# A row-wise softmax over 4096 rows of 32768: from four partitions per row to one whole row per partition

## Chip, cores and metric

One Trainium2 chip, one of its cores. The metric is device microseconds (us) of one execution; lower is better. All runs told here were with a granted clock of 1.000. In the profiles DVE is VectorE, ACT is ScalarE, and SPq is the sequencer that issues the transfers; "the page" is the summary of one profiled execution. Code is condensed, and cuts are marked with `...`.

## The reference

```
logits: (16, 256, 32768) float32, temperature = 1.0
scaled = logits / temperature
scaled = scaled - scaled.max(axis=-1, keepdims=True)
e = exp(scaled)
return e / e.sum(axis=-1, keepdims=True)      # float32
```

Flattened, that is 4096 rows of 128 KB: 537 MB in and 537 MB out. A row that was read once and stays in on-chip memory until it is scaled needs no second read, and both kernels work so.

## The kernel before

Each row is cut into four parts of 8192 elements, which lie on four neighbouring partitions. A tile is 32 rows, 128 partitions of 32 KB, or 4 MiB that lie together in memory. A tile finishes its own rows, so it can be stored as soon as it has been computed; the four partitions of a row exchange their maxima and sums by shuffles.

```
_W = 8192; _BUFS = 6; _AHEAD = 4; _CC = 4096; _SCALE_ON_DVE = {1, 4, 7}
x = xf.rearrange("n (h v) -> (n h) v", h=SPLIT)            # SPLIT = 4

def load(t):  nc.sync.dma_start(out=xs, in_=x[t * P : (t + 1) * P, :])
def store(t): nc.sync.dma_start(out=o[t * P : (t + 1) * P, :], in_=slots.pop(t))

def compute(t):
    for c in range(NCH):                                    # two pieces of 4096
        nc.vector.tensor_reduce(out=nm[:, c:c+1], in_=xc, axis=X, op=A.max, negate=True)
        nc.scalar.activation(out=xc, in_=xc, func=Exp, bias=nm[:, c:c+1], scale=inv_t,
                             accum_out=ssum[:, c:c+1])
    # ... small ops: maximum and sum over the pieces, combine() over four partitions,
    # reciprocal, factor f per piece ...
    for c in range(NCH):
        if (t * NCH + c) % 8 in _SCALE_ON_DVE:
            nc.vector.tensor_scalar_mul(out=xc, in0=xc, scalar1=f[:, c:c+1])
        else:
            nc.scalar.activation(out=xc, in_=xc, func=Copy, scale=f[:, c:c+1])

for t in range(min(_AHEAD, n_tiles)): load(t)
for t in range(n_tiles):
    compute(t); store(t)
    if t + _AHEAD < n_tiles: load(t + _AHEAD)
```

Of the kernel before, what the change touches and what calls it, by code (L numbers as in the profile page):

```python
# [1 line left out]

# [4 lines left out]


_W = 8192
_BUFS = 6  # L10
_AHEAD = 4
_CC = 4096
_SCALE_ON_DVE = {1, 4, 7}


@with_exitstack
def kernel(
    ctx: ExitStack,
    tc: tile.TileContext,
    logits: bass.AP,  # L20
    temperature: bass.AP,
    out: bass.AP,
):
    nc = tc.nc
    inv_t = 1.0 / float(temperature)
    P = nc.NUM_PARTITIONS
    fp32 = mybir.dt.float32
    Exp = mybir.ActivationFunctionType.Exp
    Copy = mybir.ActivationFunctionType.Copy
    X = mybir.AxisListType.X  # L30
    A = mybir.AluOpType

    xf = logits.flatten_outer_dims()
    of = out.flatten_outer_dims()
    N, V = xf.shape
    W = min(_W, V)
    SPLIT = V // W
    assert SPLIT * W == V and (N * SPLIT) % P == 0 and W % _CC == 0
    x = xf.rearrange("n (h v) -> (n h) v", h=SPLIT)
    o = of.rearrange("n (h v) -> (n h) v", h=SPLIT)  # L40
    n_tiles = N * SPLIT // P
    n_rounds = SPLIT.bit_length() - 1
    NCH = W // _CC

    xpool = ctx.enter_context(tc.tile_pool(name="x", bufs=_BUFS))
    spool = ctx.enter_context(tc.tile_pool(name="stats", bufs=8))
    slots = {}

    def load(t: int) -> None:
        xs = xpool.tile([P, W], fp32, tag="x", name="xs")  # L50
        slots[t] = xs
        tc.keep_in_program_order(
            nc.sync.dma_start(out=xs, in_=x[t * P : (t + 1) * P, :])
        )

    def store(t: int) -> None:
        tc.keep_in_program_order(
            nc.sync.dma_start(out=o[t * P : (t + 1) * P, :], in_=slots.pop(t))  # L58
        )

    def combine(v, op) -> None:
        for j in range(n_rounds):
            mask = [i ^ (1 << j) for i in range(32)]
            nc.vector.stream_shuffle(  # L64
                out=v[:, j + 1 : j + 2], in_=v[:, j : j + 1], mask=mask
            )
            nc.vector.tensor_tensor(  # L67
                out=v[:, j + 1 : j + 2],
                in0=v[:, j : j + 1],
                in1=v[:, j + 1 : j + 2],  # L70
                op=op,
            )

    def compute(t: int) -> None:
        xs = slots[t]
        nm = spool.tile([P, NCH], fp32, tag="nm", name="nm")
        ssum = spool.tile([P, NCH], fp32, tag="ssum", name="ssum")
        ee = spool.tile([P, NCH], fp32, tag="ee", name="ee")
        f = spool.tile([P, NCH], fp32, tag="f", name="f")
        ttj = spool.tile([P, NCH], fp32, tag="ttj", name="ttj")  # L80
        nMh = spool.tile([P, 1 + n_rounds], fp32, tag="nMh", name="nMh")
        Sh = spool.tile([P, 1 + n_rounds], fp32, tag="Sh", name="Sh")
        rS = spool.tile([P, 1], fp32, tag="rS", name="rS")

        for c in range(NCH):
            xc = xs[:, c * _CC : (c + 1) * _CC]
            nc.vector.tensor_reduce(  # L87
                out=nm[:, c : c + 1], in_=xc, axis=X, op=A.max, negate=True
            )
            if inv_t != 1.0:  # L90
                nc.vector.tensor_scalar_mul(
                    out=nm[:, c : c + 1], in0=nm[:, c : c + 1], scalar1=inv_t
                )
            nc.scalar.activation(  # L94
                out=xc,
                in_=xc,
                func=Exp,
                bias=nm[:, c : c + 1],
                scale=inv_t,
                accum_out=ssum[:, c : c + 1],  # L100
            )

        with tc.high_priority():
            nc.vector.tensor_reduce(out=nMh[:, 0:1], in_=nm, axis=X, op=A.min)  # L104
            combine(nMh, A.min)
            nc.scalar.activation(  # L106
                out=ee,
                in_=nm,
                func=Exp,
                bias=nMh[:, n_rounds : n_rounds + 1],  # L110
                scale=-1.0,
            )
            nc.vector.tensor_tensor_reduce(  # L113
                out=ttj,
                in0=ee,
                in1=ssum,
                scale=1.0,
                scalar=0.0,
                op0=A.mult,
                op1=A.add,  # L120
                accum_out=Sh[:, 0:1],
            )
            combine(Sh, A.add)
            nc.vector.reciprocal(out=rS, in_=Sh[:, n_rounds : n_rounds + 1])  # L124
            nc.scalar.activation(out=f, in_=ee, func=Copy, scale=rS)  # L125

        for c in range(NCH):
            xc = xs[:, c * _CC : (c + 1) * _CC]
            if (t * NCH + c) % 8 in _SCALE_ON_DVE:
                nc.vector.tensor_scalar_mul(out=xc, in0=xc, scalar1=f[:, c : c + 1])  # L130
            else:
                nc.scalar.activation(out=xc, in_=xc, func=Copy, scale=f[:, c : c + 1])  # L132

    for t in range(min(_AHEAD, n_tiles)):
        load(t)
    for t in range(n_tiles):
        compute(t)
        store(t)
        if t + _AHEAD < n_tiles:
            load(t + _AHEAD)  # L140


# [1 line left out]
_INS = ['logits', 'temperature']  # L144
_OUTS = [((16, 256, 32768), 'float32')]

_NUMBERS = {'temperature': 1.0}


# [26 lines left out]
```

## Time and profile before

| | before |
|---|---|
| median (range), runs at prediction time | 2506.95 us (2502.8 to 2507.95) |
| DMA queue, share of 16 engines' span | 99.6% |
| DVE, ACT busy | 63%, 65% |
| rate in the middle | 433 GB/s |

These are lines of the page of the kernel before: the span, the engines' busy time, the DMA share in tenths and the rate in 40 equal slices, the DMA queue (packets, MB, share), the chain of waits by engine, and three groups of instructions (line, engine, operation, shapes, count; busy us and mean ns; idle time just before, and its releaser).

```profile
span 2500.8 us, 4102 instructions
...
DVE 1564.4 (63%) x2400; ACT 1625.0 (65%) x929; POOL 0.2 (0%) x4
...
DMA  9999999999999999999999999999999999999997
GB/s 406 429 432 431 431 434 433 431 434 434 431 436 433 431 435 433 432 434 432 432 436 431 432 435 433 432 435 433 431 435 433 431 435 433 431 435 433 431 434 325
...
q1 hardware_dynamic: 36864, 1073.76, 99.6%
...
DMA 76%; DVE 10%; ACT 8%; another core or an unknown queue 4%; issue 0%; SPq 0%; ACTq 0%
...
L87 DVE TENSOR_REDUCE nm<-xs 128x1 f32<-128x4096 f32 x256 | 1119.6, 4414 | 432.9 <-DMA xs<-in_logits_dram 432.9
...
L132 ACT ACTIVATE xs<-xs,f 128x4096 f32<-128x4096 f32 x160 | 589.9, 3705 | 4.1
...
L130 DVE TENSOR_SCALAR xs<-xs,f 128x4096 f32<-128x4096 f32 x96 | 225.9, 2353 | 41.0 <-ACT f L125 39.7
```

The DMA row stands at 9 in all slices but the last, and the rate hardly moves: the kernel is bound by the DMA engines. DVE waits 433 us for loads, which costs nothing.

A table of windows of the same kernel has, per stretch, its length, the busy us of each engine, the clock, the DMA share and the rate.

```profile
core 0: us, DVE busy (x) ACT busy (x) POOL busy (x), PEclk, DMA share, GB/s
...
1000.00:2400.00 1400.00, 880.70 (x1350) 912.54 (x522) 0.00 (x0) 1.00 1.00 433
2475.00:2501.00 26.00, 2.30 (x1) 3.65 (x1) 0.00 (x0) 1.00 0.45 192
```

In the middle the engines move 433 GB/s at a share of 1.00; one 4 MiB transfer takes 9.68 us. The last 26 us are less than half used: the last load must be reduced, exponentiated and scaled before the last store. The Trainium skill, "DMA: Bandwidth & Descriptors", section "Where 436 GB/s comes from", gives a fabric ceiling of 435.2 GB/s; this trace agrees. (The same section says that some 358 GB/s, a core's half of its HBM stack, bind transfers between HBM and on-chip memory; with one core at work, as here, they did not.) So no change to the computation can gain much in the middle.

The timeline of one tile (start, duration, engine, line, operation) gives the length of what stands between a landed load and its store:

```profile
999.33 8.74 DVE L87 TENSOR_REDUCE nm<-xs 128x1 f32<-128x4096 f32 x2 [2.63 <-DMA xs<-in_logits_dram]
...
1013.37 0.29 ACT L125 ACTIVATE f<-ee,rS 128x2 f32<-128x2 f32 x1 [1.27 <-DVE rS L124]
1013.70 3.71 ACT L132 ACTIVATE xs<-xs,f 128x4096 f32<-128x4096 f32 x1
1013.70 2.35 DVE L130 TENSOR_SCALAR xs<-xs,f 128x4096 f32<-128x4096 f32 x1 [0.42 <-ACT f L125]
1017.43 0.34 SPq L58 DMA_DIRECT2D out_dram<-xs  x1
```

From the first reduce (999.33) to the store's issue (1017.43) are 18.1 us. Nothing waits for them, because four loads are ahead.

### The profile page before, as it was taken

How to read it: one execution, taken by the hardware profiler on the slowest of the kernel's cores; microseconds unless marked ns; L12 is line 12 of the kernel's file. 1: busy time of each engine (PE TensorE's matmuls, PEld its weight loads, DVE VectorE, ACT ScalarE, POOL GpSimd, SP SyncE). 2: the span in 40 equal slices, each digit the busy share in tenths (PEclk: the TensorE clock that was granted, in tenths of full speed). 3: DMA queues.
4: the chain of work that ended last, by engine and by line, in shares of the span. 5: the costliest groups of instructions: out<-in, count | busy, mean ns of one | idle time of the engine just before them, and what ended most of it. 6: DMA issues, size and time to landing. Idle time of an engine off the chain costs nothing.

```text
span 2500.8 us, 4102 instructions
## 1 busy us (share of the span) xinstructions
DVE 1564.4 (63%) x2400; ACT 1625.0 (65%) x929; POOL 0.2 (0%) x4
## 2 busy tenths in 40 slices
DVE  6666566666566665666666666666666666666564
ACT  6766666666666666666666666666666666666664
POOL 0000000000000000000000000000000000000000
DMA  9999999999999999999999999999999999999997
GB/s 406 429 432 431 431 434 433 431 434 434 431 436 433 431 435 433 432 434 432 432 436 431 432 435 433 432 435 433 431 435 433 431 435 433 431 435 433 431 434 325
DMA packets 36896, 1074.02 MB, mean 429 GB/s; under 512 B 4096, under 2 KB 4096, under 8 KB 4096
## 3 DMA queue, kind: packets, MB, share of 16 engines
q1 hardware_dynamic: 36864, 1073.76, 99.6%
q14 instruction: 32, 0.26, 0.0%
HBM read 536.87 MB, written 536.87 MB: 429 GB/s over the span
## 4 chain that ended last, share of the span: by engine, by line
DMA 76%; DVE 10%; ACT 8%; another core or an unknown queue 4%; issue 0%; SPq 0%; ACTq 0%
DMA xs<-in_logits_dram 47%; DMA out_dram<-xs 29%; DVE nm L87 9%; ACT xs L132 4%; ACT xs L94 4%; DVE Sh L67 0%; DVE Sh L64 0%; ACT f L125 0%; ACT ee L106 0%; DVE rS L124 0%; DVE ttj L113 0%; SPq L58 0%; DVE xs L130 0%; DVE nMh L67 0%
## 5 line engine op out<-in xcount | busy, mean ns | idle before, releaser
L87 DVE TENSOR_REDUCE nm<-xs 128x1 f32<-128x4096 f32 x256 | 1119.6, 4414 | 432.9 <-DMA xs<-in_logits_dram 432.9
L94 ACT ACTIVATE xs<-xs,nm 128x4096 f32<-128x4096 f32 x256 | 949.1, 3707 | 677.5 <-DVE nm L87 677.5
L132 ACT ACTIVATE xs<-xs,f 128x4096 f32<-128x4096 f32 x160 | 589.9, 3705 | 4.1
L113 DVE CUSTOM_DVE_ANT_0 ttj<-ee,ssum 128x2 f32<-128x2 f32 x128 | 20.5, 160 | 391.5 <-ACT ee L106 382.9
L130 DVE TENSOR_SCALAR xs<-xs,f 128x4096 f32<-128x4096 f32 x96 | 225.9, 2353 | 41.0 <-ACT f L125 39.7
L125 ACT ACTIVATE f<-ee,rS 128x2 f32<-128x2 f32 x128 | 37.8, 295 | 159.0 <-DVE rS L124 159.0
L94 ACT ACTIVATION_READ_ACCUMULATOR xs<-xs,nm 128x1 f32 x256 | 47.7, 187 | 0.0
L67 DVE TENSOR_TENSOR nMh<-nMh 128x1 f32<-128x1 f32 x256 | 40.8, 159 | 8.6
L67 DVE TENSOR_TENSOR Sh<-Sh 128x1 f32<-128x1 f32 x256 | 40.8, 159 | 8.6
L64 DVE STREAM_SHUFFLE nMh<-nMh 128x1 f32<-128x1 f32 x256 | 38.8, 151 | 0.0
L64 DVE STREAM_SHUFFLE Sh<-Sh 128x1 f32<-128x1 f32 x256 | 38.7, 151 | 0.0
L106 ACT ACTIVATE ee<-nm,nMh 128x2 f32<-128x2 f32 x128 | 35.8, 280 | 0.0
L124 DVE RECIPROCAL rS<-Sh 128x1 f32<-128x1 f32 x128 | 21.0, 164 | 4.3
L104 DVE TENSOR_REDUCE nMh<-nm 128x1 f32<-128x2 f32 x128 | 19.8, 155 | 4.3
L113 DVE DVE_READ_ACCUMULATOR2_ANT Sh<- 128x1 f32 x128 | 10.6, 83 | 0.0
L64 DVE LOAD_MASK_SELECT Sh<-Sh x256 | 3.6, 14 | 10.8
L64 DVE LOAD_MASK_SELECT nMh<-nMh x256 | 3.6, 14 | 10.8
L94 ACT ACT_TABLE_LOAD x1 | 1.3, 1283 | 13.1 <-DMA xs<-in_logits_dram 13.1
L157 POOL MEMSET const-bfloat16-1.0<- 128x1 bf16 x1 | 0.1, 101 | 0.0
L157 POOL MEMSET const-uint8-127<- 128x1 uint8 x1 | 0.1, 101 | 0.0
L157 POOL MEMSET const-float32-0.0<- 128x1 f32 x1 | 0.1, 98 | 0.2 <-issue 0.2
L157 POOL MEMSET const-float32-1.0<- 128x1 f32 x1 | 0.1, 98 | 0.0
## 6 DMA issues: line engine op xcount, KB each, us to landing
xs<-in_logits_dram SPq DMA_DIRECT2D x128, 4096.0 KB, 48.4
out_dram<-xs SPq DMA_DIRECT2D x128, 4096.0 KB, 49.6
```

Source lines behind the costliest of these rows:

```text
L64: nc.vector.stream_shuffle(out=v[:, j + 1 : j + 2], in_=v[:, j : j + 1], mask=mask)
L67: nc.vector.tensor_tensor(out=v[:, j + 1 : j + 2], in0=v[:, j : j + 1], in1=v[:, j + 1 : j + 2], op=op,)
L87: nc.vector.tensor_reduce(out=nm[:, c : c + 1], in_=xc, axis=X, op=A.max, negate=True)
L94: nc.scalar.activation(out=xc, in_=xc, func=Exp, bias=nm[:, c : c + 1], scale=inv_t, accum_out=ssum[:, c : c + 1],)
L104: nc.vector.tensor_reduce(out=nMh[:, 0:1], in_=nm, axis=X, op=A.min)
L106: nc.scalar.activation(out=ee, in_=nm, func=Exp, bias=nMh[:, n_rounds : n_rounds + 1], scale=-1.0,)
L113: nc.vector.tensor_tensor_reduce(out=ttj, in0=ee, in1=ssum, scale=1.0, scalar=0.0, op0=A.mult, op1=A.add, accum_out=Sh[:, 0:1],)
L124: nc.vector.reciprocal(out=rS, in_=Sh[:, n_rounds : n_rounds + 1])
L125: nc.scalar.activation(out=f, in_=ee, func=Copy, scale=rS)
L130: nc.vector.tensor_scalar_mul(out=xc, in0=xc, scalar1=f[:, c : c + 1])
L132: nc.scalar.activation(out=xc, in_=xc, func=Copy, scale=f[:, c : c + 1])
L157: nc = _bacc.Bacc("TRN2", target_bir_lowering=False, num_devices=1)
```

## The change

Each partition holds a whole row in four chunks of 32 KB (a *group* is 128 rows, four chunks), so no exchange between partitions is needed. All four chunks must have been exponentiated before any can be scaled and stored. Six buffers hold one and a half groups. Each scale is split between DVE (2560 columns) and ACT (1536). A transfer takes 128 pieces of 32 KB at a pitch of 128 KB. The loads of the first and last groups and the stores of the last move in half transfers, to start and end sooner. Two small edits come with it: the factors are computed on DVE instead of ACT, and the small statistics tiles have three buffers instead of eight.

```
-_W = 8192
+_SPLIT = 1
+_CW = 8192
 _BUFS = 6
-_AHEAD = 4
-_CC = 4096
-_SCALE_ON_DVE = {1, 4, 7}
+_PIECE = 4096
+_LAST_DMA = 4096
+_DVE_SHARE = 0.625
 ...
+    def load(i):
+        g, c = divmod(i, C)                                  # C = 4 chunks per group
+        for s, n in spans(CW, _LAST_DMA if g in (0, G - 1) else CW):
+            nc.sync.dma_start(out=xs[:, s : s + n],
+                in_=x[g * P : (g + 1) * P, c * CW + s : c * CW + s + n])
 ...                                       (store alike, halves in the last group only)
+            cut = int(n * _DVE_SHARE) // 512 * 512
+            nc.vector.tensor_scalar_mul(out=xs[:, s : s + cut], ...)
+            nc.scalar.activation(out=xs[:, s + cut : s + n], ..., func=Copy, ...)
 ...
+    order = [("L", i) for i in range(min(_BUFS, n_chunks))] + [("S", 0)]
+    for i in range(1, n_chunks):
+        order.append(("S", i))
+        if i + _BUFS - 1 < n_chunks:
+            order.append(("L", i + _BUFS - 1))
 ...                   (before the first "S" of a group: exps of its four chunks, then factors)
```

More of the change, by code (lines that the diff above doesn't have):

```diff
@@ L35, with spans, piece, load @@
     N, V = xf.shape
-    W = min(_W, V)
-    SPLIT = V // W
-    assert SPLIT * W == V and (N * SPLIT) % P == 0 and W % _CC == 0
-    x = xf.rearrange("n (h v) -> (n h) v", h=SPLIT)
-    o = of.rearrange("n (h v) -> (n h) v", h=SPLIT)
-    n_tiles = N * SPLIT // P
-    n_rounds = SPLIT.bit_length() - 1
-    NCH = W // _CC
+    W = V // _SPLIT
+    CW = min(_CW, W)
+    C = W // CW
+    assert W * _SPLIT == V and CW * C == W and (N * _SPLIT) % P == 0
+    x = xf.rearrange("n (h v) -> (n h) v", h=_SPLIT)
+    o = of.rearrange("n (h v) -> (n h) v", h=_SPLIT)
+    G = N * _SPLIT // P
+    n_chunks = G * C
+    n_rounds = _SPLIT.bit_length() - 1
     xpool = ctx.enter_context(tc.tile_pool(name="x", bufs=_BUFS))
-    spool = ctx.enter_context(tc.tile_pool(name="stats", bufs=8))
+    spool = ctx.enter_context(tc.tile_pool(name="stats", bufs=3))
     slots = {}
-    def load(t: int) -> None:
-        xs = xpool.tile([P, W], fp32, tag="x", name="xs")
-        slots[t] = xs
-        tc.keep_in_program_order(
-            nc.sync.dma_start(out=xs, in_=x[t * P : (t + 1) * P, :])
-        )
-    def store(t: int) -> None:
-        tc.keep_in_program_order(
-            nc.sync.dma_start(out=o[t * P : (t + 1) * P, :], in_=slots.pop(t))
-        )
+    stats = {}
+    def spans(total: int, step: int) -> list[tuple[int, int]]:
+        return [(s, min(step, total - s)) for s in range(0, total, step)]
+    def piece(g: int) -> int:
+        return _PIECE if g < G - 1 else min(_PIECE, _LAST_DMA)
+    def load(i: int) -> None:
+        g, c = divmod(i, C)
+        xs = xpool.tile([P, CW], fp32, tag="x", name="xs")
+        slots[i] = xs
+        for s, n in spans(CW, _LAST_DMA if g in (0, G - 1) else CW):
+            tc.keep_in_program_order(
+                nc.sync.dma_start(
+                    out=xs[:, s : s + n],
+                    in_=x[g * P : (g + 1) * P, c * CW + s : c * CW + s + n],
+                )
+            )
+    def store(i: int) -> None:
+        g, c = divmod(i, C)
+        xs = slots.pop(i)
+        for s, n in spans(CW, _LAST_DMA if g == G - 1 else CW):
+            tc.keep_in_program_order(
+                nc.sync.dma_start(
+                    out=o[g * P : (g + 1) * P, c * CW + s : c * CW + s + n],
+                    in_=xs[:, s : s + n],
+                )
+            )
     def combine(v, op) -> None:
@@ L72, in combine, with exps, factors @@
             )
-    def compute(t: int) -> None:
-        xs = slots[t]
-        nm = spool.tile([P, NCH], fp32, tag="nm", name="nm")
-        ssum = spool.tile([P, NCH], fp32, tag="ssum", name="ssum")
-        ee = spool.tile([P, NCH], fp32, tag="ee", name="ee")
-        f = spool.tile([P, NCH], fp32, tag="f", name="f")
-        ttj = spool.tile([P, NCH], fp32, tag="ttj", name="ttj")
+    def exps(i: int) -> None:
+        g, c = divmod(i, C)
+        xs = slots[i]
+        ps = spans(CW, piece(g))
+        K = C * len(ps)
+        if c == 0:
+            stats[g] = tuple(
+                spool.tile([P, K], fp32, tag=f"{nm}{K}", name=nm)
+                for nm in ("nm", "ssum", "ee", "f", "ttj")
+            )
+        nm, ssum = stats[g][:2]
+        for j, (s, n) in enumerate(ps):
+            k = c * len(ps) + j
+            nc.vector.tensor_reduce(
+                out=nm[:, k : k + 1], in_=xs[:, s : s + n], axis=X, op=A.max, negate=True
+            )
+            if inv_t != 1.0:
+                nc.vector.tensor_scalar_mul(
+                    out=nm[:, k : k + 1], in0=nm[:, k : k + 1], scalar1=inv_t
+                )
+            nc.scalar.activation(
+                out=xs[:, s : s + n],
+                in_=xs[:, s : s + n],
+                func=Exp,
+                bias=nm[:, k : k + 1],
+                scale=inv_t,
+                accum_out=ssum[:, k : k + 1],
+            )
+    def factors(g: int) -> None:
+        nm, ssum, ee, f, ttj = stats[g]
         nMh = spool.tile([P, 1 + n_rounds], fp32, tag="nMh", name="nMh")
@@ L83, in compute @@
         rS = spool.tile([P, 1], fp32, tag="rS", name="rS")
-        for c in range(NCH):
-            xc = xs[:, c * _CC : (c + 1) * _CC]
-            nc.vector.tensor_reduce(
-                out=nm[:, c : c + 1], in_=xc, axis=X, op=A.max, negate=True
-            )
-            if inv_t != 1.0:
-                nc.vector.tensor_scalar_mul(
-                    out=nm[:, c : c + 1], in0=nm[:, c : c + 1], scalar1=inv_t
-                )
-            nc.scalar.activation(
-                out=xc,
-                in_=xc,
-                func=Exp,
-                bias=nm[:, c : c + 1],
-                scale=inv_t,
-                accum_out=ssum[:, c : c + 1],
-            )
         with tc.high_priority():
@@ L124, in compute, with scales @@
             nc.vector.reciprocal(out=rS, in_=Sh[:, n_rounds : n_rounds + 1])
-            nc.scalar.activation(out=f, in_=ee, func=Copy, scale=rS)
-        for c in range(NCH):
-            xc = xs[:, c * _CC : (c + 1) * _CC]
-            if (t * NCH + c) % 8 in _SCALE_ON_DVE:
-                nc.vector.tensor_scalar_mul(out=xc, in0=xc, scalar1=f[:, c : c + 1])
-            else:
-                nc.scalar.activation(out=xc, in_=xc, func=Copy, scale=f[:, c : c + 1])
-    for t in range(min(_AHEAD, n_tiles)):
-        load(t)
-    for t in range(n_tiles):
-        compute(t)
-        store(t)
-        if t + _AHEAD < n_tiles:
-            load(t + _AHEAD)
+            nc.vector.tensor_scalar_mul(out=f, in0=ee, scalar1=rS)
+    def scales(i: int) -> None:
+        g, c = divmod(i, C)
+        xs = slots[i]
+        f = stats[g][3]
+        ps = spans(CW, piece(g))
+        for j, (s, n) in enumerate(ps):
+            k = c * len(ps) + j
+            cut = int(n * _DVE_SHARE) // 512 * 512
+            nc.vector.tensor_scalar_mul(
+                out=xs[:, s : s + cut], in0=xs[:, s : s + cut], scalar1=f[:, k : k + 1]
+            )
+            nc.scalar.activation(
+                out=xs[:, s + cut : s + n],
+                in_=xs[:, s + cut : s + n],
+                func=Copy,
+                scale=f[:, k : k + 1],
+            )
+    order = [("L", i) for i in range(min(_BUFS, n_chunks))] + [("S", 0)]
[3 more added lines that the diff above has]
+            order.append(("L", i + _BUFS - 1))
+    nxt = 0
+    done = -1
+    loaded = 0
+    for kind, i in order:
+        if kind == "L":
+            load(i)
+            loaded = i + 1
+        else:
+            g = i // C
+            if g > done:
+                while nxt < (g + 1) * C:
+                    assert nxt < loaded
+                    exps(nxt)
+                    nxt += 1
+                factors(g)
+                done = g
+            scales(i)
+            store(i)
 _INS = ['logits', 'temperature']
```

## The prediction

> **What bounds the kernel now.** The DMA engines. The page's second part shows them at least 90% busy in 39 of 40 slices; its third part gives the queue 99.6% of 16 engines' span, 1073.7 MB. A table of windows gives 433 GB/s at DMA share 1.00 from 100 to 2400 us. The timeline repeats one load plus one store every 19.35 to 19.40 us: 9.7 us per 4 MiB transfer. DVE (63%) and ACT (65%) have slack; the chain is 76% DMA. Little is lost at the ends: about 1.5 us idle in the first 13 us, and about 14 us in the last 26 (DMA share 0.45), where the last load is followed by reduce, exponential, factors and scale before the last store.
>
> **What the change does.**
> - Bytes and number of large transfers stay, so the floor stays near 1073.7 MB / 433 GB/s = 2480 us.
> - Removed: 512 shuffles (151 ns) and 512 combines (159 ns), 159 us of DVE; the factor chain runs 32 times, not 128. Each scale is split: DVE 2560 of 4096 columns (estimate from 2353 ns: 1.48 us), ACT 1536 (estimate from 3.7 us per 4096 and 0.28 us for two columns: 1.5 us). DVE busy about 1500 us, ACT 1360. None of this is on the critical path.
> - Added: no chunk can be stored before all four of its group are exponentiated, with six buffers; load i+5 waits until store i-1 has landed.
> - The 32 KB pieces of a transfer lie 128 KB apart.
>
> **The critical stretch.** By the new issue order, in each group the last load is followed in the queue by just one store and one load (19.4 us). In that time must fit: landing notice, two reduces and the last exponential with its accumulator (12.6 us in the old timeline), factors (about 0.9 us from the small ops), the first chunk's scale (3.05 us), issue and start. That is 16.7 us of compute; the first load's 12.27 us from issue to landing less 9.7 puts notice and start together at about 2.6 us. Sum 19.3 against 19.4: just balanced. I expect a gap of 0 to 1 us per group, 0.4 typical, times 31: about 12 us.
>
> **Ends.** At the start six loads (58 us) cover the first group's compute (first store near 54 us). At the end, half-size transfers and four stores in a row leave about 7 us idle instead of 15: 8 us gained.
>
> **Spacing.** The Trainium skill, "DMA: Bandwidth & Descriptors", section "Latency and other measured facts", has copies of 16 KiB pieces at a 512 KiB pitch at 207 GB/s per direction against 214 full, far less from 2 MiB up. 128 KB is below its smallest figure; no run here shows it yet. I allow 0 to 1%, 0.2% (5 us) typical.
>
> **Sum.** 2507 - 8 + 12 + 5 = 2516, shaded to 2512 us because the balance may leave no gap. Range 2488 to 2548. Faster by over 2% would need more than the DMA ceiling: 1%. Within 2%: 88%. Slower: 11%.
>
> **What would show it.** DMA share near 1.00 in the middle windows at 430 to 433 GB/s; DVE near 1500 and ACT near 1360 us; stores' wait for DVE or ACT ends, once per group, within about 1 us of the queue draining; less idle in the last 26 us. If DMA share is 1.00 but GB/s below 430, pieces are slower; if share falls, gaps are the cause.
>
> **What would make it wrong.** Pieces 128 KB apart several per cent slower; notice-to-start above 2.6 us under load, or engines out of step, so that gaps reach 2 us per group (over 60 us); scales on DVE and ACT together slower than alone; or a scheduler order that puts a later group's reduces before scales.

## The result

| | before | after |
|---|---|---|
| median (range) | 2505.12 us (2502.8 to 2507.95), 4 runs | 2580.66 us (2579.22 to 2581.61), 4 runs |
| ratio of the runs, 95% interval | | 1.0301 (1.0283 to 1.0318) |
| DVE, ACT busy, us | 1564, 1625 | 1518, 1359 |
| rate in the middle | 433 GB/s | 416 GB/s |

A ratio is the mean time of one kernel's runs over that of the other's of the same rounds, so it is not quite the ratio of the medians. The change made the kernel 3% slower, outside the predicted range.

The same lines of the page after the change:

```profile
span 2579.0 us, 2299 instructions
...
DVE 1517.9 (59%) x672; ACT 1359.3 (53%) x801; POOL 0.2 (0%) x4
...
DMA  9999999999999999999999999999999999999999
GB/s 415 431 430 425 413 421 416 419 413 412 415 423 416 412 410 420 414 422 412 416 417 422 418 411 412 418 422 417 411 416 416 423 417 415 410 416 423 418 410 384
...
q1 hardware_dynamic: 38592, 1073.76, 98.9%
...
DMA 96%; ACT 1%; DVE 1%; SPq 1%; issue 0%; ACTq 0%
...
L107 DVE TENSOR_REDUCE nm<-xs 128x1 f32<-128x4096 f32 x256 | 1119.7, 4413 | 901.4 <-DMA xs<-in_logits_dram 901.4
...
L163 ACT ACTIVATE xs<-xs,f 128x1536 f32<-128x1536 f32 x256 | 378.9, 1562 | 24.5 <-DVE f L150 24.5
L160 DVE TENSOR_SCALAR xs<-xs,f 128x2560 f32<-128x2560 f32 x256 | 377.3, 1548 | 1.1
```

DVE and ACT came out as predicted (1518 and 1359 us against 1500 and 1360), and the DMA row still says 9 everywhere. But the rate is near 416, and the chain is 96% DMA: the DMA engines are occupied, and deliver less. The windows agree, and show that the end improved:

```profile
1000.00:2400.00 1400.00, 831.44 (x373) 745.67 (x441) 0.00 (x0) 1.00 0.99 416
2545.00:2579.00 34.00, 2.34 (x2) 2.45 (x2) 0.00 (x0) 1.00 0.95 402
```

The timeline at the end of one group: the reduces of its last chunk, the scales, the issue of the group's first store (L75) and of the load behind it (L64):

```profile
1076.36 8.74 DVE L107 TENSOR_REDUCE nm<-xs 128x1 f32<-128x4096 f32 x2 [11.62 <-DMA xs<-in_logits_dram]
...
1089.84 7.40 DVE L160 TENSOR_SCALAR xs<-xs,f 128x2560 f32<-128x2560 f32 x5
1089.89 7.44 ACT L163 ACTIVATE xs<-xs,f 128x1536 f32<-128x1536 f32 x5 [0.77 <-DVE f L150]
1092.96 0.33 SPq L75 DMA_DIRECT2D out_dram<-xs  x1
1093.39 0.38 SPq L64 DMA_DIRECT2D xs<-in_logits_dram  x1
```

From the first reduce on the group's last chunk (1076.36) to the issue of the group's first store (1092.96) are 16.60 us; the prediction had 16.7. Now the DMA engines around that store:

```profile
1082.50:1092.20 9.70, 5.70 (x8) 8.46 (x7) 0.00 (x0) 1.00 1.00 432
1092.20:1093.70 1.50, 1.50 (x2) 1.50 (x2) 0.00 (x0) 1.00 0.07 27
1093.70:1102.00 8.30, 8.30 (x7) 8.03 (x6) 0.00 (x0) 1.00 1.03 439
1102.00:1104.10 2.10, 2.10 (x1) 0.00 (x0) 0.00 (x0) 1.00 0.97 265
1104.10:1111.20 7.10, 6.18 (x2) 4.69 (x3) 0.00 (x0) 1.00 1.03 443
1111.20:1115.00 3.80, 0.00 (x0) 2.91 (x2) 0.00 (x0) 1.00 1.00 302
1115.00:1124.70 9.70, 6.72 (x2) 2.27 (x1) 0.00 (x0) 1.00 0.99 429
```

The view counts a piece in the stretch in which it starts, so that a share can exceed 1.00. The second line is a gap: hardly a piece starts (share 0.07), and with the pieces still running from before, the engines were 29% busy. The fourth and sixth lines are something else: the share is 0.97 and 1.00, yet the rates are 265 and 302 GB/s. In these two stretches the engines are never idle, and each piece takes longer. They lie at the end of the group's first store and at the end of the load behind it. The other lines run at the full rate.

### An account in pieces

The trace records every piece that an engine moved, with start, duration and size. A piece of 32 KB takes 1.213 us nearly always, a half piece 0.611 us. Summed over all pieces and divided by 16 engines, in us:

```
                                        before     after
pieces at their usual duration          2484.2    2485.1
what pieces took beyond that               4.7      63.4
engines idle, first 60 us                  2.2       2.0
engines idle, middle                       0.0      27.7
engines idle, last 60 us                  14.9       6.4
sum                                     2506.0    2584.6
span of the profile                     2500.8    2579.0
slow pieces (over 1.3 us per 32 KB)        164      1649
```

Neighbouring pieces of an engine overlap by some 3 ns, so each sum exceeds its span by 5 to 6 us. The difference of the sums is 78.6 us, that of the spans 78.2: the middle gaps cost 28, slow pieces 59, and the end gives back 8.5.

Each transfer ends on each engine with one 4-byte write, which raises the semaphore (the counter on which the compute engines wait). So sorted by time each 16 of these close one transfer, as long as the engines are less than one transfer apart; that holds for this kernel. It gives, for one group after the change (us; excess, here and in the table of margins below, is what the slow pieces took beyond their usual duration, per engine):

```
transfer              issued    first engine done  last engine done  margin  excess
last load of group   1045.59        1072.86            1075.99        17.59    0.09
store                1046.02        1082.54            1085.67        26.84    0.00
load                 1065.74        1092.22            1096.21        16.80    0.00
first store of group 1092.96        1104.13            1105.90        -0.74    0.78
load                 1093.39        1114.95            1117.61        10.74    1.14
store                1095.89        1124.64            1127.29        19.06    0.00
```

*Margin* is the time from the issue of a transfer to the end of what stood before it on the first engine to finish. At -0.74 the store came after the first engine had nothing left.

### The profile page after: what moved, and what is told of

Its sections match the earlier page's. It is cut to its first block, busy times and chain, and to the rows that moved or that the text cites. A ratio compares the mean times of both kernels' runs of the same rounds, so it can differ in the third digit from the quotient of the medians.

```text
span 2579.0 us, 2299 instructions
## 1 busy us (share of the span) xinstructions
DVE 1517.9 (59%) x672; ACT 1359.3 (53%) x801; POOL 0.2 (0%) x4
## 4 chain that ended last, share of the span: by engine, by line
DMA 96%; ACT 1%; DVE 1%; SPq 1%; issue 0%; ACTq 0%
DMA out_dram<-xs 62%; DMA xs<-in_logits_dram 34%; ACT xs L163 1%; DVE nm L107 1%; SPq L64 1%; ACT xs L114 0%; ACTq L224 0%; DVE f L150 0%; ACT ee L131 0%; DVE rS L149 0%; SPq L75 0%; DVE ttj L138 0%; DVE Sh L138 0%; ACTq L163 0%
## 5 line engine op out<-in xcount | busy, mean ns | idle before, releaser
L163 ACT ACTIVATE xs<-xs,f 128x1536 f32<-128x1536 f32 x256 | 378.9, 1562 | 24.5 <-DVE f L150 24.5
L160 DVE TENSOR_SCALAR xs<-xs,f 128x2560 f32<-128x2560 f32 x256 | 377.3, 1548 | 1.1
L138 DVE CUSTOM_DVE_ANT_0 ttj<-ee,ssum 128x8 f32<-128x8 f32 x32 | 5.4, 167 | 123.6 <-ACT ee L131 123.6
L131 ACT ACTIVATE ee<-nm,nMh 128x8 f32<-128x8 f32 x32 | 9.1, 285 | 0.0
L150 DVE TENSOR_SCALAR f<-ee,rS 128x8 f32<-128x8 f32 x32 | 7.4, 230 | 1.1
L149 DVE RECIPROCAL rS<-Sh 128x1 f32<-128x1 f32 x32 | 5.3, 164 | 1.1
L129 DVE TENSOR_REDUCE nMh<-nm 128x1 f32<-128x8 f32 x32 | 5.2, 161 | 1.1
L138 DVE DVE_READ_ACCUMULATOR2_ANT Sh<- 128x1 f32 x32 | 2.6, 83 | 0.0
```

The costliest lines, as they stand in the source:

```text
L129: nc.vector.tensor_reduce(out=nMh[:, 0:1], in_=nm, axis=X, op=A.min)
L131: nc.scalar.activation(out=ee, in_=nm, func=Exp, bias=nMh[:, n_rounds : n_rounds + 1], scale=-1.0,)
L138: nc.vector.tensor_tensor_reduce(out=ttj, in0=ee, in1=ssum, scale=1.0, scalar=0.0, op0=A.mult, op1=A.add, accum_out=Sh[:, 0:1],)
L149: nc.vector.reciprocal(out=rS, in_=Sh[:, n_rounds : n_rounds + 1])
L150: nc.vector.tensor_scalar_mul(out=f, in0=ee, scalar1=rS)
L160: nc.vector.tensor_scalar_mul(out=xs[:, s : s + cut], in0=xs[:, s : s + cut], scalar1=f[:, k : k + 1])
```

## The experiments

Eleven kernels were run, each four times, but two_stores, before_ahead2, pairs_delay24, pairs_delay96 and deep only twice; one execution of each was traced. "Slow" counts pieces over 1.3 us per 32 KB, "excess" is as in the account, "middle idle" leaves out the first and last 60 us of the trace. The expectations of the first two submissions counted 32 KB pieces only (after: 1571 slow, 57.6 us in slow pieces). `contig` and `before_apart` mix rows on purpose; the comparison passed even so, presumably since rows of this input have nearly the same sum, and nothing rests on it.

| run | median us | ratio to before | slow | excess us | middle idle us |
|---|---|---|---|---|---|
| (after) | 2580.66 | 1.0301 | 1649 | 63.4 | 27.7 |
| contig | 2576.72 | 1.0287 | 1636 | 62.2 | 27.2 |
| half4 | 2528.46 | 1.0097 | 1057 | 34.1 | 0.5 |
| before_apart | 2509.25 | 1.0019 | 133 | 4.2 | 0.0 |
| half4_delay24 | 2590.09 | 1.0339 | 1701 | 64.2 | 30.1 |
| pairs | 2496.33 | 0.9970 | 265 | 6.6 | 0.0 |
| two_stores | 2557.21 | 1.0212 | 1494 | 59.7 | 10.5 |
| half4_store0 | 2521.01 | 1.0055 | 956 | 24.7 | 0.4 |
| before_ahead2 | 2744.16 | 1.0959 | 3059 | 109.9 | 117.8 |
| pairs_delay24 | 2506.18 | 1.0006 | 328 | 8.7 | 7.9 |
| pairs_delay96 | 2609.32 | 1.0417 | 1489 | 60.8 | 47.7 |
| deep | 2542.38 | 1.0150 | 1966 | 44.2 | 1.8 |

### Is it the spacing? contig and before_apart

`contig` keeps the changed schedule and takes contiguous transfers:

```
-   in_=x[g * P : (g + 1) * P, c * CW + s : c * CW + s + n]
+   in_=xt[i * P : (i + 1) * P, s : s + n]        # xt: rows of 8192; the store alike
```

> Wrong results on purpose: the changed kernel's schedule, but transfer i takes the 4 MiB that lie together, as before the change. In the trace of the changed kernel a 32 KB piece takes 1.213 us nearly always; 1571 pieces took over 1.3 us (57.6 us per DMA engine in sum, before: 4.2), nearly all about 10 and 20 us after the gap that opens once per group. Theory A (spacing: pieces 128 KB apart are slow): the slow pieces vanish, the gap stays, about 2520 us. Theory B (the gap of about 1 us once per group starts all 16 engines in step, and engines in step pay about 1 us at each of the next two changes between storing and loading): nothing changes, 2575 to 2585 us, about 1500 slow pieces.

`before_apart` keeps the old schedule and takes pieces 128 KB apart:

```
-   in_=x[t * P : (t + 1) * P, :]
+   in_=xf[t//4*P : (t//4+1)*P, t%4*W : (t%4+1)*W]      # the store alike
```

> Wrong results on purpose: the kernel before the change with its schedule untouched, but each transfer takes 128 pieces of 32 KB that lie 128 KB apart. Theory A: about 57 us slower than before, 2560 us. Theory B: the same as before within 0.3%, 2500 to 2512 us.

Measured: 2576.72 and 2509.25 us. Their middle windows, contig first:

```profile
1000.00:2400.00 1400.00, 831.57 (x374) 747.25 (x441) 0.00 (x0) 1.00 0.99 417
```

```profile
1000.00:2400.00 1400.00, 878.11 (x1340) 908.57 (x518) 0.00 (x0) 1.00 1.00 433
```

417 GB/s with contiguous transfers, 433 GB/s with pieces 128 KB apart: the spacing costs nothing that matters (before_apart's ratio is 1.0019), and theory A falls.

### Is it the gap? half4 and half4_delay24

`half4` halves the last load of every group, so the first reduce starts half a transfer earlier:

```
-   for s, n in spans(CW, _LAST_DMA if g in (0, G - 1) else CW):
+   for s, n in spans(CW, _LAST_DMA if g in (0, G - 1) or c == C - 1 else CW):
```

> The changed kernel with the last load of every group in two halves, so that its first reduce starts 4.85 us earlier and the group's first store is ready before the queue drains; the spacing stays 128 KB. Theory A: only the gaps go (31 of about 1 us), the slow pieces stay, 2540 to 2555 us. Theory B: gaps and slow pieces both go, 2490 to 2505 us, fewer than 300 slow pieces.

`half4_delay24` adds idle work to the same stretch:

```
+   for _ in range(24):
+       nc.vector.tensor_scalar_mul(out=f, in0=f, scalar1=1.0)
```

> half4 with 24 idle copies of the factors (about 6 us) put back into the critical stretch of every group, so that the gap comes back with another cause (about 2 us; the slack of half4 is estimated at 3.5 to 4.5 us). Theory B: the slow pieces come back with it, over 1200, and each group loses gap plus 1.9 us: 2595 to 2630 us. Theory A: the number of slow pieces is that of half4, whatever that is; time half4 plus 31 gaps of 2 us.

The middle of half4:

```profile
1000.00:2400.00 1400.00, 839.62 (x366) 749.71 (x440) 0.00 (x0) 1.00 1.00 426
```

The share is 1.00, the rate still below 433. half4 took 2528.46 us, which neither theory had expected. The gaps went (0.5 us idle in the middle), but 1057 slow pieces stayed, so an idle engine is not needed for them. Nor is step enough: in the table of one group, 15 of 16 engines still finish the second store within 0.72 us of each other, and the change of direction behind it has no slow piece. Theory B falls as it was stated. half4_delay24 took 2590.09 us, 5 us under theory B's range. Theory A's time (half4 plus 62 us) fits by chance, for the slow pieces, which A left as they were, rose from 1057 to 1701. Of its 30 us of middle gaps 8 are one gap near 60 us, in the first group, where only six loads stand in the queue. Its middle:

```profile
1000.00:2400.00 1400.00, 903.53 (x805) 741.07 (x438) 0.00 (x0) 1.00 0.99 417
```

What half4 showed instead is a measure. Its first groups had margins of 5.9, 3.6 and 2.7 us and no loss to speak of; then the engines drifted apart, from 1.2 to 5.4 us between first and last, the margin shrank to about 1.3, and slow pieces came. The compute waits for the *last* engine of a load, while the queue runs dry on the *first*. Over the groups' first stores of after, contig, half4 and half4_delay24 between 110 and 2380 us, the excess in that store and the load behind it is:

```
margin us        groups   store   load behind   sum
below 0              67    0.79       1.10      1.89
0    to 0.5           6    0.73       1.10      1.83
0.5  to 1            13    0.54       1.07      1.61
1    to 1.25          7    0.36       0.96      1.31
1.25 to 1.5          10    0.19       0.78      0.97
1.5  to 2             6    0.11       0.52      0.63
2    to 3             2    0.03       0.18      0.21
above 3               2    0.00       0.08      0.09
```

So theory C: a transfer that joins the queue less than about 2 us before the first engine has finished what stood there makes pieces slow at the next changes between storing and loading, by up to 1.9 us, whether or not a gap opens. How far the engines are apart is not what decides: at a margin near 1 us, four stores of half4_delay24 with engines 0.7 to 0.9 us apart cost 1.6 to 1.7 us, nine of half4 with engines 5.5 to 5.9 us apart 1.2 to 1.5.

### Only the order: pairs

```
-    order = [("L", i) for i in range(min(_BUFS, n_chunks))] + [("S", 0)]
-    for i in range(1, n_chunks):
-        order.append(("S", i))
-        if i + _BUFS - 1 < n_chunks:
-            order.append(("L", i + _BUFS - 1))
+    order = [("L", i) for i in range(min(_BUFS, n_chunks))]
+    for i in range(0, n_chunks, 2):
+        order += [("S", i), ("S", i + 1)]
+        order += [("L", k) for k in (i + _BUFS, i + _BUFS + 1) if k < n_chunks]
```

> The changed kernel with only the order of issue altered: two stores, then two loads, so that after a group's last load two stores and two loads (38.8 us) still stand in the queue instead of one of each (19.4). What the first four runs leave (theory C): a store that joins the queue less than about 2 us before the first DMA engine has finished what stood there (margin) costs up to 0.75 us at the next change from storing to loading and 1.1 us at the next change back, besides any gap; neither spacing nor engines in step alone do it. Theory C: margin over 8 us at each group's first store, fewer than 300 slow pieces, no gaps, 2488 to 2502 us. If slow pieces belong to the group structure itself (scales and reduces in bursts), they stay, 2535 us or more.

Measured: 2496.33 us, ratio 0.9970 (0.9955 to 0.9985; clear of noise), no gap in the middle, 265 slow pieces. After 150 us the store that follows the loads joins with 11.7 to 17.8 us of margin, the loads with at least 2.2. Its windows:

```profile
300.00:1000.00 700.00, 426.30 (x190) 381.05 (x224) 0.00 (x0) 1.00 1.00 432
1000.00:2400.00 1400.00, 861.79 (x380) 768.62 (x454) 0.00 (x0) 1.00 1.00 432
2470.00:2494.00 24.00, 0.00 (x0) 0.00 (x0) 0.00 (x0) 1.00 0.73 311
```

The bytes, buffers, spacing, instructions and split scales are those of the change; only the order of issue differs, and the 3% loss is a 0.3% gain. So the rest of the change, taken together, does no harm. This version beats both kernels, the old one by 0.3%.

### Do the slow pieces follow the changes of direction? two_stores

```
+    for i in range(C, n_chunks, C):
+        j = order.index(("S", i))
+        if order[j + 1][0] == "L":
+            order[j + 1], order[j + 2] = order[j + 2], order[j + 1]
```

> The changed kernel with each group's first load and second store exchanged (store, store, load, load, store, ...), the tail behind the group's last load as it was, so the margin stays below 0. Theory C: the slow pieces move with the changes of direction: none at the end of the first store (about 9 us after its start), then at the end of the second store (about 19 us) and at the end of the second load (about 38 us); 2570 to 2590 us. If the bursts of scales and reduces on DVE and ACT cause them, they stay at about 9 and 19 us after the first store's start.

A group whose first store was issued at 446.10, in windows that start with that store's end (it began near 447):

```profile
456.70:465.00 8.30, 6.72 (x2) 5.35 (x3) 0.00 (x0) 1.00 1.03 442
465.00:467.30 2.30, 0.00 (x0) 2.26 (x2) 0.00 (x0) 1.00 1.10 328
467.30:477.00 9.70, 0.00 (x0) 0.00 (x0) 0.00 (x0) 1.00 1.00 432
477.00:484.40 7.40, 6.40 (x2) 1.95 (x1) 0.00 (x0) 1.00 1.06 443
484.40:487.60 3.20, 2.35 (x1) 2.68 (x3) 0.00 (x0) 1.00 0.90 297
487.60:497.00 9.40, 7.88 (x2) 6.35 (x3) 0.00 (x0) 1.00 0.97 418
```

The rate sinks at the end of the second store (328) and at the end of the second load (297), and nowhere else. The slow pieces moved with the order, so bursts of scales and reduces, which stayed, do not cause them. The time, 2557 us, is 13 us below the expectation. The margin rose to about +0.3, because the engines were about 2 us apart before each group's first store instead of 3, so the gaps cost 10.5 us instead of 27.7.

### More margin by other means: half4_store0 and deep

`half4_store0` also halves each group's first store:

```
-   for s, n in spans(CW, _LAST_DMA if g == G - 1 else CW):
+   for s, n in spans(CW, _LAST_DMA if g == G - 1 or c == 0 else CW):
```

> half4 with each group's first store in two halves as well, so that the first half is issued about 1.5 us earlier: margin about 2.8 us instead of 1.3. Theory C: of half4's 952 slow pieces fewer than 350 stay, 2497 to 2512 us against 2528. Without the margin law: 2528 us.

Measured: 2521.01 us (2504.13 to 2526.5), 956 slow pieces: the expectation was missed, and the four runs differ by more than any others here. The margin began at 7.5 us, but the engines drifted 6 to 8 us apart, and from 590 us on it lay between 0.6 and 2.2. Most of the 1.5 us was gained and lost again.

`deep` has half-size chunks and twice the buffers:

```
-_CW = 8192
-_BUFS = 6
+_CW = 4096
+_BUFS = 12
```

> The changed kernel with chunks of 16 KB per partition and twelve buffers, otherwise the order as in the change: same bytes in flight, but a half-size last load and about 29 us of queue behind it, so the margin grows by another way than pairs. Theory C: no gaps, few slow pieces; the 16 KB pieces take 0.611 us instead of half of 1.213, about 9 us more (estimate: 0.0045 us times 65536 pieces over 16 engines is 18 us at most): 2495 to 2515 us.

Measured: 2542.38 us, missed by 27 (two executions, 2537.0 and 2547.77; the trace is of the second). Its windows show when:

```profile
300.00:1000.00 700.00, 428.44 (x189) 381.25 (x225) 0.00 (x0) 1.00 1.01 431
1000.00:1600.00 600.00, 357.33 (x159) 320.91 (x189) 0.00 (x0) 1.00 1.01 431
1700.00:2400.00 700.00, 399.63 (x173) 355.83 (x210) 0.00 (x0) 1.00 1.00 408
```

431 GB/s until 1600 us, 408 after 1700, with the same instructions throughout. Here it is the loads, which wait for a store to land, whose margin shrinks as the engines drift apart: 5.3 us at 300, 4.0 near 1200, about 2 from 1700 on. From 3 to 6 us 163 loads have no excess (0.00 us); from 2.25 to 2.5 it is 0.17, from 1.8 to 2.0 it is 0.63 us. So the law is not one of groups, nor of stores alone. The smaller pieces cost 18 us besides (65536 pieces at 0.611 us come to 2502.7 us).

### Without groups: before_ahead2

```
-_AHEAD = 4
+_AHEAD = 2
```

> The kernel before the change with two loads ahead instead of four: right results, each transfer contiguous, no groups; after a load lands only 19.4 us of queue remain against 18.1 us of compute plus about 2.6 us of notice and start. Theory C: slow pieces appear here too, at nearly every tile, more than 2000, and gaps; 2560 to 2720 us. If they need the change's groups or its split scales: no slow pieces, only gaps of about 0.6 us per tile, under 2590 us.

Measured: 2744.16 us, just above the range, with 3059 slow pieces (109.9 us) and 138 us of idle engines up to the last 60 us (20.5 of them in the first 60). The old kernel with right results and contiguous tiles shows the same slow pieces once its queue is as short: they need nothing of the change. The gaps were under-estimated. The margin orders the loss here too, in the late store itself: 36 stores with a margin below 0 have 0.70 us of excess, 27 at 1 to 2 us have 0.37, and 30 above 3 us have 0.00, although the engines are nearly in step throughout (0.6 us apart, 2 at most). Its middle:

```profile
1000.00:2400.00 1400.00, 808.19 (x1233) 835.40 (x478) 0.00 (x0) 1.00 0.96 396
```

### A late first store in the good order: pairs_delay24 and pairs_delay96

The edit is that of half4_delay24, with 24 and 96 copies on top of `pairs`.

> pairs with the same 24 idle copies (4.9 us in half4_delay24's trace) in every group's critical stretch that cost half4 62 us. Theory C: a group's first store still joins with more than 5 us of margin, so they cost nothing: 2493 to 2501 us, no gaps, fewer than 350 slow pieces.

> pairs with 96 idle copies (19.7 us): stretch 16.7 + 19.7 + 2.6 us for notice and start = 39.0 us against the 38.8 us that stand behind a group's last load, as near to balance as the changed kernel's 19.3 against 19.4. Theory C: gaps and slow pieces come back, over 1000 of these, at the two changes of direction after each group's first store, 2550 to 2630 us. If pairs escapes them by its order alone: about 2496 us.

pairs_delay24 took 2506.18 us, 5 above its range. One early window and the middle of it:

```profile
60.00:70.00 10.00, 10.00 (x7) 9.48 (x6) 0.00 (x0) 1.00 0.18 76
...
1000.00:2400.00 1400.00, 928.50 (x811) 763.89 (x450) 0.00 (x0) 1.00 1.00 432
```

The middle stays at 432 GB/s. The loss is one gap near 60 us (share 0.18): in the *first* group only six loads stand in the queue, and 4.9 us more of compute outlast them. That start had been left out of the expectation. pairs_delay96, 2609.32 us, is as expected in time and slow pieces: 1489 of these, at the end of each group's second store and second load. But of its 48 us of middle gaps 31 are again the first group's, which the expectation had left out. So the good order is not immune; it only has a margin to spend.

## Why the prediction was wrong

- Right: the bound (DMA), the floor, DVE and ACT busy times, the compute stretch (16.60 us against 16.7), the start, and the end: 8.5 us less idle against the 8 predicted.
- Right: the spacing. 0.2% was allowed, before_apart measured 0.19%, and contig stands within 0.14 points of the changed kernel.
- Wrong: "Sum 19.3 against 19.4: just balanced", and from it "a gap of 0 to 1 us per group, 0.4 typical". Two terms were mis-sized. Notice and start were put at 2.6 us from the first load's 12.27 us, but that load had slow pieces of its own (0.58 us per engine) and is no clean measure: the last engine ended at 1075.99 and the reduce began at 1076.36, 0.37 us, and after a dry queue the first piece starts 0.83 us after the issue began, 1.2 us together. And the distance between the first and the last engine was left out: 3.13 us at that load. For the first engine the sum is 3.13 + 0.37 + 16.60 + 0.83 = 20.9 us against 19.36, a gap of 1.6 us; over all engines and groups it is 27.7 us instead of 12, or 0.9 us for each of 31 groups. The sum came as near as it did by luck: the start was put 1.4 us too long, which hid half of the distance left out. The prediction named "engines out of step" as a risk, but gave it no term.
- Wrong by omission, and the larger part: "if share falls, gaps are the cause" and "if DMA share is 1.00 but GB/s below 430, pieces are slower" were right as tests, but slow pieces were expected only from spacing (5 us). What came was 59 us of slow pieces from a transfer that joined the queue too late. That a late transfer costs up to 1.9 us beyond any gap was in no part of the sum: this missing term is the step that failed most. With the measured terms it closes: 2505 - 8.5 + 28 + 59 = 2583 against a median of 2581, where 2505 is the old median.
- Open: what in the DMA engines makes the pieces slow. The loss sets in near 2 us of margin, and start (0.83 us) plus one piece (1.21 us) is 2.04 us, which would fit an engine that wants the next transfer's description one piece ahead. That is only argued. It does not explain why the loss falls on the next two changes of direction, 10 and 20 us later, and not on the restart. Two cases near the start lie outside the table: in after, half4, pairs and two_stores the very first change from loading to storing, near 60 us, had 0.4 to 0.7 us of excess at a margin of 6.4 to 6.8 us; and the first store of the kernel before, at a margin of 1.7 us, cost 1.7 us with the load behind it, where the table has 0.63. Why the engines drift apart was not studied either.

## What to carry to other kernels

In a kernel bound by DMA, count how much work stands in the queue when the next transfer is issued, and count it for the first engine to run dry, while compute waits for the last one. Here, once the start was over, 2 us of remaining work was too little and 3 us was enough, and with the same buffers an order of two stores and two loads gave that margin, worth 3.3%. Where the DMA share stays at 1.00 and the rate falls, look at the durations of single pieces before suspecting addresses.

## What the Trainium skill lacked or had wrong

- "DMA: Bandwidth & Descriptors", section "Latency and other measured facts", gives row pitches from 512 KiB up. A pitch of 128 KB with 32 KB pieces is missing: 433 GB/s in both directions together, ratio 1.0019 to contiguous transfers.
- The same section gives about 600 ns to the first byte on the hardware path. Here the first piece after a dry queue starts 0.83 us after the start of the issue (0.82 to 0.84 in 25 stores of the changed kernel), which itself lasts 0.33 us, so about 0.5 us after its end.
- The same page, section "Anatomy of one DMA — SWDGE (gpsimd) path", puts a fixed cost of about 2.0 us on a DMA of that path, mostly after the last byte. On the hardware path of this kernel the reduce began 0.37 us after the recorded end of the last engine's write; carrying 2 us over would have been wrong here. Whether a piece's recorded time already holds part of that cost is not shown.
- The same page, section "Why a DMA increments its semaphore by 16 and not by 1", says that the engines of a DMA finish independently, and the runs agree, but no page says how far apart they drift: 1 to 4 us after the change, about 6 in pairs, and 15 to 17 late in the kernel before, by the events of each transfer's own semaphore. There it does no harm: until its last load the margin stays above 19 us.
- No page has the cost of a queue that runs nearly dry: 1.9 us of slow pieces per engine at the next two changes between storing and loading, falling to 0.2 us at 2 to 3 us of margin in this kernel and its variants.
